# Sixteen of 22 chunks of the last down projection by Strassen's algorithm

## The chip, the core and the metric

The kernel runs as one program on one core of a Trainium2 chip. The core has a matrix engine (PE in the profile; its weight loads are listed apart as PEld), a vector engine (DVE), an activation engine (ACT), a general-purpose engine (POOL), and DMA queues, all of which are issued here from the sync engine's queue (SPq). The engines run beside each other and wait for one another through semaphores. Each takes its instructions in the order in which they were laid out when the program was built. The metric is the time of one execution on the device in microseconds (us); less is better.

## The reference

Two layers of a decoder trunk on 512 tokens of 1024 features. What matters here is the end of the second layer and the norm behind it, all in float32:

```
        h = rms_norm(x, norm2_g[layer]) * (1 + scale2) + shift2
        u = causal_depthwise_conv(h @ w_up[layer], conv_w[layer], conv_b[layer])
        u_gate, u_val = jnp.split(u, 2, axis=-1)
        x = x + gate2 * ((jax.nn.silu(u_gate) * u_val) @ w_down[layer])
    return rms_norm(x, final_g)
```

The activations silu(u_gate) * u_val are 512 tokens by 2816 features; w_down is 2816 by 1024.

## The kernel before

**Precision.** [...] A product of two operands is then three matmuls (high by high, low by high, high by low). `split` makes the parts of a tile of weights: ACT copies it into the high tile `wh` (L566), DVE subtracts into the low tile `wl` (L567). `hilo` does the same for activations (L703 on ACT, L705 or L707 on DVE). There are three buffers for raw weights (`st`) and two each for `wh` and `wl`.

**The feed-forward stage.** `ffn` runs over 22 chunks of 128 features (`NF`). For each it makes two up projections of 24 matmuls (L650 to L652), the three-tap convolution (L1366 to L1368, ACT then DVE), the gate (L1371 to L1373), and with `hilo` the two tiles `act` (high and low, 128 features by 512 tokens). Beside it run the sums of the gate modulation, whose weights are loaded from `w_mod` into tiles `wr`, and `by_tokens`, which loads the residual stream into tiles `x`, transposes it on PE (L535) and writes it back by tokens.

**The last stage.** `last_residual` computes the down projection with tokens on the partitions. A half is 512 of the 1024 output columns; each half is a call of `proj_steps`: for each pair of chunks one tile of weights of 256 rows by 512 columns (512 KB) is loaded and split, and each of four blocks of 128 tokens takes three matmuls per chunk into its own PSUM bank. That is 22 x 4 x 3 = 264 matmuls of 512 columns a half, all at L607 and, for the last eight chunks of the second half, at L581 to L583, where the weights stay in tiles `wr` and the blocks are finished one after the other. `ev` then evacuates a block: DVE multiplies by the gate row (L1330) and adds to the residual (L1331), ACT squares and sums (L1332), DVE multiplies by the norm's gain (L1334 in the first half, L1339 in the second); in the second half follow the small steps of the norm (L1336, L1337 on DVE, L1338 on POOL), the scaling (L1340 on ACT, L1341 on DVE) and two DMAs of the output (L1343).

**Order.** The build lays out each engine's instructions itself, from the program's order and its own estimate of when each can start; the few places that are fixed by hand (`in_order`) are not in the last stage. An engine that stands at a wait holds everything behind it.

Of the kernel before, what the change touches and what calls it, by code (L numbers as in the profile page):

```python
# [23 lines left out]
DFF = 2816  # L24
NF = DFF // P
NU = 2 * NF
NCMP = 31
NEG = -1e30
EPS = 1e-6
# [4 lines left out]
EARLY = (0, NF, 1, NF + 1)  # L34
# [61 lines left out]
def together(*gens):  # L96

    gens = list(gens)
    while gens:
        for g in list(gens):  # L100
            if next(g, gens) is gens:
                gens.remove(g)


class Trunk:
# [5 lines left out]
                   s16=4, hid=1, hidT=1, w2=1, vc=1, den=8, nm=8),  # L111
        "ME": dict(yy=20, m=16),
        "FF": dict(act=44, x=9, wr=16),
        "ST": dict(macc=8, ms=20, ws=16),
    }
    ALL = (mybir.EngineType.PE, mybir.EngineType.DVE, mybir.EngineType.Activation)
# [1193 lines left out]
                M[1].append(lo)  # L1310
        return M

    def last_residual(self, src, Hs, row, rtag):
# [5 lines left out]
        rows, ss = {}, self.t("x", [P, NB, 3])  # L1319
        for half in range(2):  # L1320

            def ev(b, p):
                if not rows:
                    rows["gate"] = self.row_bc(row, "x")
                    rows["gain"] = self.row_bc(io["final_g"], "x")
                x = self.x[b, half]
                s = ss[:, b]
                for i, c in enumerate((slice(0, 256), slice(256, 512)) if half else (slice(0, 512),)):
                    t = self.t("tmp", [P, 512])
                    nc.vector.tensor_tensor(t[:, c], p[:, c], rows["gate"][half][:, c], op=ALU.mult)  # L1330
                    nc.vector.tensor_add(x[:, c], x[:, c], t[:, c])  # L1331
                    nc.scalar.activation(t[:, c], x[:, c], AF.Square, scale=D ** -0.5, accum_out=s[:, half + i:half + i + 1])  # L1332
                if half == 0:
                    nc.vector.tensor_tensor(x, x, rows["gain"][0], op=ALU.mult)  # L1334
                    return
                nc.vector.tensor_tensor(s[:, 0:1], s[:, 0:1], s[:, 1:2], op=ALU.add)  # L1336
                nc.vector.tensor_scalar(s[:, 0:1], s[:, 0:1], s[:, 2:3], EPS, op0=ALU.add, op1=ALU.add)  # L1337
                nc.gpsimd.tensor_tensor(s[:, 0:1], s[:, 0:1], self.nhalf, op=ALU.pow)  # L1338
                nc.vector.tensor_tensor(x, x, rows["gain"][1], op=ALU.mult)  # L1339
                nc.scalar.activation(self.x[b, 0], self.x[b, 0], AF.Copy, scale=s[:, 0:1])  # L1340
                nc.vector.tensor_scalar(x, x, s[:, 0:1], None, op0=ALU.mult)  # L1341
                for e in range(2):
                    nc.sync.dma_start(io["out"][0, b * P:(b + 1) * P, e * 512:e * 512 + 512], self.x[b, e])  # L1343

            yield from self.proj_steps(src, [(half * 512, half * 512 + 512)], Hs, ev, tags=("mm", "at")[half],
                                       resident=8 * half, rtag=rtag, order=((0,), (1,), (2,), (3,)))
# [5 lines left out]
    def ffn(self, l, H, act, early):  # L1352
        nc, io = self.nc, self.io
        W = io["w_up"][l]
        for j in range(NF):
            u2 = self.t("wr", [P, 2, S])
            for e, col in enumerate((j, NF + j)):
                p = early.get(col)
                if p is None:
                    p = self.pt("mm")  # L1360
                    with self.in_order(self.ALL) if j == 2 else nullcontext():
                        w = self.w_tok(W, 0, KD, [(col * P, col * P + P)], P)
                    for k in range(KD):
                        self.mm3f(p, w[0][:, k], w[1][:, k], H[0][k], H[1][k], k == 0, k == KD - 1)
# [12 lines left out]
            act[1].append(lo)  # L1377
            yield

    def run(self):  # L1380
        nc, io = self.nc, self.io
        self.setup()
        AB = self.new_AB()
        for l in range(DEPTH):
            with self.scope("Y"):
                if l == 0:

                    with self.scope("ST"):
# [95 lines left out]
            with self.scope("FF"):  # L1484
                act = ([], [])
                gate2, row = self.new_gate(), self.gate_row() if l + 1 == DEPTH else None
# [5 lines left out]
                mods, ffn = chain(*mods), self.ffn(l, H, act, dict(zip(EARLY, early)))  # L1492
                for j, _ in enumerate(ffn):
                    for _ in range(2 if j in (4, 8, 12, 16, 20) else 1):
                        next(mods, None)
                    next(back, None)
                if l + 1 < DEPTH:
                    pc = []
                    gate1, ABn = self.new_gate(), self.new_AB()
                    mods = chain(self.mod_gate(l + 1, 0, gate1, None, 1024, ("wr", "wr")), self.mod_affine(l + 1, 1, ABn, 0, 1024, ("wr", "wr")))  # L1500
                    H = self.add_norm(io["w_down"][l], act, gate2, AB, "x", 1, 2, lambda H: self.cmp_proj(l + 1, H, ("wr", "wr"), pc), mods)
                    together(mods)
                else:
                    together(self.last_residual(io["w_down"][l], act, row, "wr"))


@with_exitstack
# [27 lines left out]
```

## Time and profile before

| | |
|---|---|
| time, median of 3 runs | 1721.5 us (1721.31 to 1725.55) |
| the profiled execution's own time | 1719.86 us |
| its span, first to last instruction | 1717.8 us |
| PE busy in the span | 1673.8 us (97%) |
| DVE busy | 1195.0 us (70%) |
| ACT busy | 837.3 us (49%) |
| last stage, first matmul to the end of the last | 1590.3 to 1710.1 us |
| from there to the end of the span | 7.6 us |

A matmul is shown busy for longer than the time until the next one starts, since they overlap; what a matmul costs in a dense stretch is the distance between starts. The same holds for DVE and ACT to a lesser degree, so their instructions are counted here by that distance too. [...]

### The profile page before, as it was taken

What the parts mean: (1) busy time and instruction counts of PE and PEld (TensorE: products, weight loads), DVE (VectorE), ACT (ScalarE), POOL (GpSimd) and SP (SyncE); (2) the same over time, 40 slices, a digit from 0 to 9 for tenths busy, and PEclk for the clock granted to TensorE, in tenths of its full rate; (3) what the DMA queues carried; (4) which work ended last, traced back from release to release, by engine and by line L of the source; (5) the groups of instructions that cost most, each with busy time, mean ns of one, the idle gap of its engine ahead of it and who ended that gap; (6) DMA issues with size and microseconds to landing.
All of it is one profiled execution on the core that took longest, in us unless ns stands there. A gap on an engine that the chain in (4) does not pass through costs nothing.

```text
span 1717.8 us, 23192 instructions
## 1 busy us (share of the span) xinstructions
PE 1673.8 (97%) x8469; PEld 1417.4 (83%) x8469; DVE 1195.0 (70%) x2278; ACT 837.3 (49%) x1638; POOL 58.1 (3%) x112
## 2 busy tenths in 40 slices
PE   6999999999999999999999999999999999999998
PEld 4799977878788888887789998778788988888886
DVE  6777768877858888776566646688876686666343
ACT  5455446777434444442334546467754444444222
POOL 3300001000000000000000000100000000000000
PEclk9999999999999999999999999999999999999999
DMA  9547432111544454467534241221146353433322
GB/s 303 172 142 235 136 111 59 49 44 56 172 153 160 159 159 151 156 199 245 186 89 121 81 121 60 53 65 41 43 140 191 127 175 108 144 95 108 134 95 85
DMA packets 274352, 220.09 MB, mean 128 GB/s; under 512 B 25481, under 2 KB 236081, under 8 KB 273983
## 3 DMA queue, kind: packets, MB, share of 16 engines
q1 hardware_dynamic: 273663, 217.57, 40.9%
q8 instruction: 66, 1.08, 0.2%
q10 hardware_dynamic: 576, 1.05, 0.2%
q14 instruction: 47, 0.39, 0.1%
HBM read 205.87 MB, written 12.71 MB: 127 GB/s over the span
## 4 chain that ended last, share of the span: by engine, by line
PE 86%; DVE 5%; DMA 3%; ACT 3%; issue 1%; SPq 0%; POOL 0%; POOLq 0%; DVEq 0%; ACTq 0%
PE pmm L607 20%; PE pmm L650 15%; PE pmm L651 15%; PE pmm L652 15%; PE pat L607 2%; PE pat L1191 2%; DMA wr<-in_w_mod_dram 2%; PE pat L1208 2%; PE pat L652 1%; PE pat L650 1%; PE pat L651 1%; ACT p L699 1%; PE pat L821 1%; DVE wl L567 1%; PE pat L581 1%
## 5 line engine op out<-in xcount | busy, mean ns | idle before, releaser
L567 DVE TENSOR_TENSOR wl<-st,wh 128x1024 fp32r<-128x1024 f32 (+3 forms) x269 | 284.2, 1058 | 194.0 <-ACT wh L566 110.1
L566 ACT ACTIVATE wh<-st 128x1024 fp32r<-128x1024 f32 (+3 forms) x269 | 249.0, 927 | 328.5 <-PE pmm L651 161.1
L650 PE MATMUL pmm<-h,wh 128*128 128x512 f32 x896 | 354.8, 396 | 0.1
L652 PE MATMUL pmm<-h,wl 128*128 128x512 f32 x896 | 350.4, 391 | 1.0 <-DVE wl L567 1.0
L651 PE MATMUL pmm<-h,wh 128*128 128x512 f32 x896 | 349.8, 390 | 0.0
L607 PE MATMUL pmm<-wh,h 128*128 128x512 f32 (+1 forms) x832 | 215.6, 396 | 3.5 <-DVE a L1008 2.1
L652 PEld LDWEIGHTS pmm<-h,wl 128*128 128x128 f32 x896 | 168.2, 188 | 37.9 <-DVE wl L567 2.5
L650 PEld LDWEIGHTS pmm<-h,wh 128*128 128x128 f32 x896 | 168.4, 188 | 32.9 <-ACT wh L566 0.8
L651 PEld LDWEIGHTS pmm<-h,wh 128*128 128x128 f32 x896 | 168.5, 188 | 32.2
L607 PEld LDWEIGHTS pmm<-wh,h 128*128 128x128 f32 x832 | 170.5, 246 | 17.2 <-DVE a L1008 3.8
L607 PE MATMUL pmm<-wl,h 128*128 128x512 f32 (+1 forms) x416 | 104.9, 385 | 0.0
L607 PEld LDWEIGHTS pmm<-wl,h 128*128 128x128 f32 x416 | 85.8, 245 | 5.9
L703 ACT ACTIVATE act<-wr 128x512 fp32r<-128x512 f32 x44 | 27.8, 632 | 110.7 <-DVE wr L1373 110.6
L699 ACT ACTIVATE p<-p,nm 128x128 f32<-128x128 f32 (+3 forms) x128 | 70.8, 554 | 21.1 <-DVE nm L697 20.3
L244 DVE SCALAR_TENSOR_TENSOR wr<-wr,silc,wr 128x1024 f32<-128x1024 f32 x49 | 62.7, 1280 | 13.8 <-DMA wr<-in_w_mod_dram 13.5
L697 DVE CUSTOM_DVE_ANT_0 p<-pat,cst 128x128 f32<-128x128 f32 (+2 forms) x192 | 61.3, 371 | 14.2 <-PE pat L583 8.1
L1366 ACT ACTIVATE wr<-pmm,cols 128x512 f32<-128x512 f32 x88 | 66.7, 763 | 6.9 <-PE pmm L652 5.7
L650 PE MATMUL pmm<-act,wh 128*128 128x512 f32 (+1 forms) x186 | 69.3, 373 | 0.6 <-DVE x L465 0.6
L652 PE MATMUL pmm<-act,wl 128*128 128x512 f32 (+1 forms) x186 | 69.2, 372 | 0.2 <-DVE wl L567 0.2
L651 PE MATMUL pmm<-act,wh 128*128 128x512 f32 (+1 forms) x186 | 69.0, 371 | 0.0
L1367 DVE SCALAR_TENSOR_TENSOR wr<-pmm,cols,wr 128x511 f32<-128x511 f32 x88 | 65.2, 744 | 3.9 <-ACT wr L1366 3.6
L1371 ACT ACTIVATE tmp<-wr 128x512 f32<-128x512 f32 x44 | 27.8, 633 | 81.3 <-DVE wr L1368 65.6
(379 smaller groups left out, 3133.8 us busy)
## 6 DMA issues: line engine op xcount, KB each, us to landing
st<-in_w_up_dram SPq DMA_DIRECT2D x80, 512.0 KB, 3.8
st<-in_w_in_dram SPq DMA_DIRECT2D x124, 256.0 KB, 2.9
wr<-in_w_mod_dram SPq DMA_DIRECT2D x56, 512.0 KB, 5.1
st<-in_w_down_dram SPq DMA_DIRECT2D x38, 512.0 KB, 4.7
st<-in_w_in_dram SPq DMA_DIRECT2D x26, 512.0 KB, 3.4
mss<-in_w_mod_dram SPq DMA_DIRECT2D x48, 256.0 KB, 2.9
ms<-in_w_mod_dram SPq DMA_DIRECT2D x16, 512.0 KB, 6.5
st<-in_w_out_dram SPq DMA_DIRECT2D x16, 512.0 KB, 3.3
```

Source lines behind the costliest of these rows:

```text
L244: nc.vector.scalar_tensor_tensor(acc, w[:, k - k0], self.sc[:, k:k + 1], acc, op0=ALU.mult, op1=ALU.add)
L566: self.nc.scalar.activation(hi, st, AF.Copy)
L567: self.nc.vector.tensor_sub(lo, st, hi.bitcast(F32))
L607: self.nc.tensor.matmul(ps[b][:, :N], H[x][k0 + e][:, s], w[y][:, e, :], start=k0 + e + i == 0, stop=k0 + e + i == nk + 1)
L650: nc.tensor.matmul(out, wh, hh, start=first, stop=False)
L651: nc.tensor.matmul(out, wh, hl, start=False, stop=False)
L652: nc.tensor.matmul(out, wl, hh, start=False, stop=last)
L697: nc.vector.tensor_tensor_reduce(out=pout, in0=ps, in1=mask, scale=-0.125, scalar=3e38, op0=ALU.add, op1=ALU.min, accum_out=negm)
L699: nc.scalar.activation(pout, pout, AF.Exp, bias=negm, scale=-1.0, accum_out=den)
L1191: nc.tensor.transpose(p[:, h * P:(h + 1) * P], src(h), self.ident)
L1366: nc.scalar.activation(u, p, AF.Identity, scale=self.cwc(l, 2, col), bias=self.cbc(l, col))
L1367: nc.vector.scalar_tensor_tensor(u[:, 1:], p[:, :S - 1], self.cwc(l, 1, col), u[:, 1:], op0=ALU.mult, op1=ALU.add)
```

## The change

Of the 22 chunks, the first 16 (`KH` = 8 twice) now go through Strassen's algorithm in Winograd's form. The activations of these chunks are cut into four quarters: by halves of the 16 chunks and by halves of the 512 tokens. The weights are cut likewise: by halves of the chunks and of the output columns. Seven products of sums of quarters, instead of eight products of quarters, give the result. A product is 8 chunks x 2 blocks x 3 = 48 matmuls of 512 columns. The six chunks that are left (`remainder`) are computed as before, 72 matmuls a half of the columns, into the same or into separate PSUM banks.

The parts that it consists of:

- In the feed-forward stage the first 16 chunks are stored unsplit in tiles `ra`, and their `hilo` is dropped. `quarter_sums`, run beside it, makes sums of quarters on DVE, splits the first product's operand (tiles `ah`), and loads four pairs of weight tiles to make their difference `t3` (the order listings call these tiles `t`). The factor one half of the gate moves into the gate row.
- In the last stage a weight tile serves 12 matmuls in a product, not 24, and 24 still in the remainders. Operands of the six other products are split there by `hilo`, two groups of four chunks each, into four buffers `ah`. Products t1, t2 and -t4 need a DVE addition or subtraction for every weight tile, t1 two loads for each.
- The results of products are copied or added on ACT and DVE (`m1`, `m7`, `u3`) and evacuated by `residual`, which is `ev` for one block. The sequence of PE is: products 11, t3, 21, the first remainder, products t2, t1, -t4, the second remainder, product 22.

The core of the diff:

```diff
+    def quarter_sums(self, W):
...
+        for j in range(NF):
+            if j % 3 == 1 and len(self.t3) < KH // 2:
+                s = len(self.t3)
+                t = self.w_quarter(W, 1, 1, s, "t3")
+                nc.vector.tensor_sub(t, t, self.w_quarter(W, 0, 1, s, "wr"))
+                self.t3.append(t)
+            for g, end in enumerate(range(3, KH, 4)):
+                a, z = self.ra[0][g], self.ra[1][g]
+                if j == end:
+                    self.a11.append(self.split_group(a[:, :, h0]))
+                if j == KH + end:
+                    s1 = self.t("sa", [P, 4, S // 2])
+                    nc.vector.tensor_add(s1, a[:, :, h1], z[:, :, h1])
+                    nc.vector.tensor_sub(a[:, :, h1], a[:, :, h0], a[:, :, h1])
+                    nc.vector.tensor_sub(a[:, :, h0], s1, a[:, :, h0])
...
+        def weights(name, s):
+            if name in ("11", "21", "22"):
+                return self.w_quarter(W, int(name[0]) - 1, int(name[1]) - 1, s, "st")
+            if name == "t1":
+                w = self.w_quarter(W, 0, 1, s, "st")
+                nc.vector.tensor_sub(w, w, self.w_quarter(W, 0, 0, s, "wr"))
+                return w
+            if name == "t2":
+                nc.vector.tensor_add(t3[s], t3[s], self.w_quarter(W, 0, 0, s, "st"))
+            if name == "-t4":
+                nc.vector.tensor_sub(t3[s], self.w_quarter(W, 1, 0, s, "st"), t3[s])
+            return t3[s]
+        def mms(ps, blocks, a, w, n, first, last=False):
+            for i, (x, y) in enumerate(((0, 0), (1, 0), (0, 1))):
+                for k in range(n):
+                    for b in blocks:
+                        nc.tensor.matmul(ps[b], a[x](k, b), w[y][:, k], ...)
+        def product(ps, A, name, first):
+            A = list(A)
+            for s in range(KH // 2):
+                a = operand(A, s)
+                w = self.split(weights(name, s), [P, 2, S])
+                mms(ps, range(2), a, w, 2, first and s == 0, s == KH // 2 - 1)
...
+        product(p1, A12, "21", False)
+        pr = pair("at")
+        remainder(p1 + pr, 0, (False, True))
+        for b in range(2):
+            t = self.t("tmp", [P, S])
+            nc.vector.tensor_tensor(t, pr[b], gate[0], op=ALU.mult)
+            nc.vector.tensor_add(self.x[2 + b, 0], self.x[2 + b, 0], t)
+        for b in range(2):
+            residual(b, 0, p1[b], 0)
+        product(p7, quarter(0, h0), "t2", False)
...
+        product(p5, self.s1, "t1", True)
...
+        product(p7, A22, "-t4", False)
+        for b in range(2):
+            nc.vector.tensor_add(m1[b], p7[b], m1[b])
+            residual(2 + b, 0, m1[b], 0)
+        pr = pair("at")
+        remainder(p5 + pr, 1, (False, True))
+        for b in range(2):
+            nc.vector.tensor_add(u3[b], pr[b], u3[b])
+            residual(2 + b, 1, u3[b], 1)
+            t = self.t("tmp", [P, S])
+            nc.vector.tensor_tensor(t, m7[b], gate[1], op=ALU.mult)
+            nc.vector.tensor_add(self.x[b, 1], self.x[b, 1], t)
+        ws, ops, A12 = [], [], list(A12)
+        for s in range(KH // 2):
+            ops.append(operand(A12, s))
+            ws.append(self.split(weights("22", s), [P, 2, S], ("wr", "wr") if s else ("wh", "wl")))
+            if s < 1:
+                mms(p5, range(2), ops[s], ws[s], 2, False)
+        for b in range(2):
+            for s in range(1, KH // 2):
+                mms(p5, (b,), ops[s], ws[s], 2, False, s == KH // 2 - 1)
+            residual(b, 1, p5[b], 1)
...
-            nc.vector.tensor_tensor(uv, uv, t, op=ALU.mult)
-            hi, lo = self.t("act", [P, S], F32R), self.t("act", [P, S], F32R)
-            self.hilo(uv, hi, lo, 0.5)
-            act[0].append(hi)
-            act[1].append(lo)
+            if raw and j < 2 * KH:
+                nc.vector.tensor_tensor(raw(j), uv, t, op=ALU.mult)
+            else:
+                nc.vector.tensor_tensor(uv, uv, t, op=ALU.mult)
+                hi, lo = self.t("act", [P, S], F32R), self.t("act", [P, S], F32R)
+                self.hilo(uv, hi, lo, 1.0 if raw else 0.5)
```

Where instructions now stand. On DVE, before the change, at the end of the first half: the evacuation of the first half's blocks (`pmm` to `tmp`, then `h`) with a weight split (`wl`) among it.

```order
L1334 TENSOR_TENSOR h_15004<-h_15004,x_15355 128x512
L1331 TENSOR_TENSOR h_15008<-h_15008,tmp_15369 128x512
L1330 TENSOR_TENSOR tmp_15374<-pmm_15020,x_15351 128x512
L567 TENSOR_TENSOR wl_15416<-st_15413,wh_15415 128x1024
L1334 TENSOR_TENSOR h_15008<-h_15008,x_15355 128x512
```

On DVE, after the change, at the end of the first remainder: `pat` and `pmm` are the four finished banks; `wl_15374` is the low part of product t2's second weight tile, and the row ahead of the eight evacuation rows makes a weight tile of product t1.

```order
L1379 TENSOR_TENSOR st_15489<-st_15489,wr_15491 128x1024
L1453 TENSOR_TENSOR tmp_15331<-pat_15239,x_14993 128x512
L1453 TENSOR_TENSOR tmp_15334<-pat_15240,x_14993 128x512
L1454 TENSOR_TENSOR h_14984<-h_14984,tmp_15331 128x512
L1454 TENSOR_TENSOR h_14988<-h_14988,tmp_15334 128x512
L1427 TENSOR_TENSOR tmp_15337<-pmm_15003,x_14993 128x512
L1427 TENSOR_TENSOR tmp_15342<-pmm_15004,x_14993 128x512
L1428 TENSOR_TENSOR h_14976<-h_14976,tmp_15337 128x512
L1428 TENSOR_TENSOR h_14980<-h_14980,tmp_15342 128x512
L569 TENSOR_TENSOR wl_15374<-t_2933_13621,wh_15373 128x1024
```

All eight evacuation rows of the first remainder stand ahead of the second weight's low part.

On ACT, before the change, in the last stage there are only weight copies in a row (`wh`), one for each 24 matmuls:

```order
L566 ACTIVATE wh_15263<-st_15261 128x1024
L566 ACTIVATE wh_15293<-st_15291 128x1024
L566 ACTIVATE wh_15323<-st_15321 128x1024
L566 ACTIVATE wh_15385<-st_15383 128x1024
L566 ACTIVATE wh_15415<-st_15413 128x1024
```

On ACT, after the change, in product -t4: `wh_15542`, `15561`, `15584`, `15603` are its four weight tiles, `ah_15577` the high part of its second operand group, `ah_15763` that of the first operand group of product 22, the last one.

```order
L568 ACTIVATE wh_15542<-t_2889_13357 128x1024
L705 ACTIVATE ah_15577<-ra_13300 128x1024
L568 ACTIVATE wh_15561<-t_2933_13621 128x1024
L705 ACTIVATE ah_15763<-ra_13299 128x1024
L568 ACTIVATE wh_15584<-t_2983_13900 128x1024
L568 ACTIVATE wh_15603<-t_3019_14136 128x1024
```

The operand of product 22, which takes an `ah` buffer that product -t4 still reads, stands ahead of -t4's third weight tile.

## Rows read from the trace of the kernel before

**Rows 1.** The page, busy time, share of the span and instructions of each engine

```profile
PE 1673.8 (97%) x8469; PEld 1417.4 (83%) x8469; DVE 1195.0 (70%) x2278; ACT 837.3 (49%) x1638; POOL 58.1 (3%) x112
```

**Rows 2.** Stretches: busy us and counts by engine, granted clock, DMA share, GB/s

```profile
1375.00:1590.30 215.30, 215.30 (x964) 177.58 (x963) 152.03 (x186) 96.82 (x129) 0.00 (x0) 1.00 0.41 126
1590.30:1650.20 59.90, 59.90 (x266) 49.41 (x265) 17.54 (x18) 13.79 (x14) 0.00 (x0) 1.00 0.34 122
1650.20:1710.20 60.00, 59.90 (x265) 49.26 (x263) 26.73 (x46) 17.12 (x32) 2.72 (x3) 1.00 0.24 83
```

**Rows 3.** Chain that ended last, in order of time: start us, us, what

```profile
1590.30 59.96 PE pmm L607 x264
1650.26 38.08 PE pat L607 x168
```

**Rows 4.** Waits, 1560 to the end: waiter <- releaser: us in total, times, longest

```profile
ACT wh L566 <- PE pmm L607: 42.7, 10, 4.4
DVE wl L567 <- PE pmm L607: 37.6, 9, 4.2
```

**Rows 5.** DVE's timeline in the last stage: start us, us, line, operation

```profile
1648.94 1.29 DVE L1330 TENSOR_TENSOR tmp<-pmm,x 128x512 f32<-128x512 f32 x2 [2.80 <-PE pmm L607]
1650.14 1.29 DVE L1331 TENSOR_TENSOR h<-h,tmp 128x512 f32<-128x512 f32 x2
1651.35 0.69 DVE L1330 TENSOR_TENSOR tmp<-pmm,x 128x512 f32<-128x512 f32 x1
...
1656.89 1.22 DVE L567 TENSOR_TENSOR wl<-st,wh 128x1024 fp32r<-128x1024 f32 x1
1658.03 0.68 DVE L1334 TENSOR_TENSOR h<-h,x 128x512 f32<-128x512 f32 x1
```

**Rows 6.** ACT's timeline in the last stage

```profile
1670.24 1.06 ACT L566 ACTIVATE wh<-st 128x1024 fp32r<-128x1024 f32 x1 [4.33 <-PE pat L607]
```

**Rows 7.** DVE's timeline from the last matmul to the end

```profile
1710.14 0.76 DVE L1330 TENSOR_TENSOR tmp<-pat,x 128x256 f32<-128x256 f32 x2 [1.59 <-PE pat L583]
1710.81 0.75 DVE L1331 TENSOR_TENSOR h<-h,tmp 128x256 f32<-128x256 f32 x2
1711.86 0.16 DVE L1336 TENSOR_TENSOR x<-x 128x1 f32<-128x1 f32 x1 [0.30 <-ACT tmp L1332]
...
1713.51 0.49 DVE L1341 TENSOR_SCALAR h<-h,x 128x512 f32<-128x512 f32 x1 [0.44 <-POOL x L1338]
```

**Rows 8.** DMA issues of the last stage: count, KB each, median us to landing

```profile
st<-in_w_down_dram SPq DMA_DIRECT2D x18, 512.0 KB, 3.5
```

**Rows 9.** Groups by line and form in the feed-forward stage: busy us, mean ns | idle

```profile
L567 DVE TENSOR_TENSOR wl<-st,wh 128x1024 fp32r<-128x1024 f32 x39 | 47.8, 1225 | 35.7 <-ACT wh L566 35.7
L707 DVE SCALAR_TENSOR_TENSOR act<-wr,act 128x512 fp32r<-128x512 f32 x20 | 13.8, 691 | 12.6 <-ACT act L703 12.6
L703 ACT ACTIVATE act<-wr 128x512 fp32r<-128x512 f32 x20 | 12.6, 632 | 50.3 <-DVE wr L1373 50.3
```

**Rows 10.** All of PE's waits from 1350 to 1717 us

```profile
PE pat L535 <- DMA x<-xd: 1.2, 2, 0.7
```

**Rows 11.** PE's timeline in the first 60 us, matmuls behind a wait

```profile
30.67 6.44 PE L607 MATMUL pmm<-ws,h 128*128 128x512 f32 x20 [1.91 <-ACT h L703]
42.97 5.78 PE L607 MATMUL pmm<-ws,h 128*128 128x512 f32 x24 [2.80 <-ACT h L703]
```

**Rows 12.** Stretches in the first 60 us, same columns as rows 2

```profile
10.00:20.00 10.00, 9.41 (x67) 8.32 (x68) 8.47 (x22) 4.81 (x13) 2.09 (x4) 1.00 1.12 349
30.00:35.00 5.00, 4.33 (x12) 3.42 (x13) 5.00 (x10) 5.00 (x17) 4.61 (x7) 0.66 0.79 223
45.00:50.00 5.00, 5.00 (x24) 4.13 (x23) 4.86 (x10) 4.36 (x13) 3.48 (x6) 1.00 0.75 274
50.00:55.00 5.00, 2.40 (x16) 2.08 (x14) 3.99 (x15) 4.41 (x11) 2.00 (x4) 0.98 0.61 164
```

More of the change, by code (lines that the diff above doesn't have):

```diff
@@ L1318, in last_residual @@
                 self.load_x(b, half)
[L1319 to L1346, printed above, removed]
@@ new lines, in last_residual @@
+        ss = self.t("x", [P, NB, 3])
+        gate, gain = self.row_bc(row, "x"), self.row_bc(io["final_g"], "x")
+        for g in gate:
+            nc.vector.tensor_scalar(g, g, 0.5, None, op0=ALU.mult)
+        h0, h1 = slice(0, S // 2), slice(S // 2, S)
+        quarter = lambda kh, c: [x[:, :, c] for x in self.ra[kh]]
+        t3 = self.t3
+        def weights(name, s):
[4 more added lines that the diff above has]
+                nc.vector.tensor_sub(w, w, self.w_quarter(W, 0, 0, s, "wr"))
+                return w
+            if name == "t2":
[3 more added lines that the diff above has]
+            return t3[s]
@@ new lines, in mms, with operand @@
+        def mms(ps, blocks, a, w, n, first, last=False):
+            for i, (x, y) in enumerate(((0, 0), (1, 0), (0, 1))):
+                for k in range(n):
+                    for b in blocks:
+                        nc.tensor.matmul(ps[b], a[x](k, b), w[y][:, k], start=first and k + i == 0, stop=last and k + i == n + 1, skip_group_check=True)
+        def operand(A, s):
+            g, o = s // 2, s % 2 * 2
+            if s % 2 == 0:
+                A[g] = A[g] if isinstance(A[g], tuple) else self.split_group(A[g])
+            return [lambda k, b, x=x: x[:, o + k, b * P:(b + 1) * P] for x in A[g]]
@@ new lines, in product, with remainder @@
+        def product(ps, A, name, first):
[4 more added lines that the diff above has]
+                mms(ps, range(2), a, w, 2, first and s == 0, s == KH // 2 - 1)
+        def remainder(ps, nh, first):
+            n = NF - 2 * KH
+            for k in range(0, n, 2):
+                st = self.t("st", [P, 2, S])
+                r = (2 * KH + k) * P
+                nc.sync.dma_start(st, W[r:r + 2 * P, nh * S:nh * S + S].rearrange("(k p) c -> p k c", p=P))
+                a = [lambda e, b, x=x: x[k + e][:, b * P:(b + 1) * P] for x in rest]
+                w = self.split(st, [P, 2, S])
+                for blocks, new in zip((range(2), range(2, NB)), first):
+                    mms(ps, blocks, a, w, 2, new and k == 0, k == n - 2)
@@ new lines, in last_residual, with residual @@
+        pair = lambda tag: [self.pt(tag) for _ in range(2)]
+        copy = lambda ps: [self.copied(p) for p in ps]
+        def residual(b, half, p, last):
+            x, s = self.x[b, half], ss[:, b]
+            for i, c in enumerate((slice(0, 256), slice(256, 512)) if last else (slice(0, 512),)):
+                t = self.t("tmp", [P, 512])
+                nc.vector.tensor_tensor(t[:, c], p[:, c], gate[half][:, c], op=ALU.mult)
+                nc.vector.tensor_add(x[:, c], x[:, c], t[:, c])
+                nc.scalar.activation(t[:, c], x[:, c], AF.Square, scale=D ** -0.5, accum_out=s[:, last + i:last + i + 1])
+            if not last:
+                nc.vector.tensor_tensor(x, x, gain[half], op=ALU.mult)
+                return
+            nc.vector.tensor_tensor(s[:, 0:1], s[:, 0:1], s[:, 1:2], op=ALU.add)
+            nc.vector.tensor_scalar(s[:, 0:1], s[:, 0:1], s[:, 2:3], EPS, op0=ALU.add, op1=ALU.add)
+            nc.gpsimd.tensor_tensor(s[:, 0:1], s[:, 0:1], self.nhalf, op=ALU.pow)
+            nc.vector.tensor_tensor(x, x, gain[half], op=ALU.mult)
+            nc.scalar.activation(self.x[b, 1 - half], self.x[b, 1 - half], AF.Copy, scale=s[:, 0:1])
+            nc.vector.tensor_scalar(x, x, s[:, 0:1], None, op0=ALU.mult)
+            for e in range(2):
+                nc.sync.dma_start(io["out"][0, b * P:(b + 1) * P, e * 512:e * 512 + 512], self.x[b, e])
@@ new lines, in last_residual @@
+        A12, A22 = quarter(1, h0), quarter(1, h1)
+        p1, p7 = pair("mm"), pair("mm")
+        product(p1, self.a11, "11", True)
+        m1 = copy(p1)
+        product(p7, quarter(0, h1), "t3", True)
+        m7 = copy(p7)
+        product(p1, A12, "21", False)
[5 more added lines that the diff above has]
+            nc.vector.tensor_add(self.x[2 + b, 0], self.x[2 + b, 0], t)
@@ new lines, in last_residual @@
+        for b in range(2):
+            residual(b, 0, p1[b], 0)
+        product(p7, quarter(0, h0), "t2", False)
+        u3 = [self.t("h", [P, S]) for _ in range(2)]
+        for b in range(2):
+            nc.vector.tensor_add(u3[b], p7[b], m1[b])
+            nc.vector.tensor_sub(m7[b], u3[b], m7[b])
+        p5 = pair("at")
+        product(p5, self.s1, "t1", True)
+        for x, y in zip(A12, quarter(0, h0)):
+            nc.vector.tensor_sub(x, x, y)
+        for b in range(2):
+            nc.vector.tensor_add(u3[b], p5[b], u3[b])
@@ L1491, in run @@
                 back = self.by_tokens("x") if l + 1 == DEPTH else iter(())
-                mods, ffn = chain(*mods), self.ffn(l, H, act, dict(zip(EARLY, early)))
+                mods, ffn = chain(*mods), self.ffn(l, H, act, dict(zip(EARLY, early)), raw)
                 for j, _ in enumerate(ffn):
@@ L1496, in run @@
                     next(back, None)
+                    next(sums, None)
                 if l + 1 < DEPTH:
@@ L1503, in run @@
                 else:
-                    together(self.last_residual(io["w_down"][l], act, row, "wr"))
+                    self.last_residual(io["w_down"][l], act, row)
 @with_exitstack
```

34 lines of the change are left out of this document (31 added, 3 removed).

## Prediction

> **What bounds the kernel now.** The page comes first: PE is busy for 97% of the span [rows 1], which says little by itself, because matmuls overlap in this listing. So the last stage is read next, by itself. In its two halves PE is busy throughout and DVE for 29% and 45% [rows 2]. The chain that ended last shows what a matmul costs there: 264 of them take 59.96 us, one piece with no gap, so 0.227 us each [rows 3]; the second half begins at 1650.26 and its first evacuation behind the last matmul at 1710.14 [rows 3, 7], the same 0.227. The waits agree: ACT and DVE wait for PE, 4.4 and 4.2 us at a time, to give back the buffers `wh` and `wl` [rows 4]; PE itself waited from 1350 us on only twice, 1.2 us together, at the start of the feed-forward stage [rows 10]. So the last stage is 528 matmuls long, then 7.6 us of norm and output. What the reader is to see: each matmul taken away is worth 0.227 us as long as ACT and DVE keep ahead, and they now have much room. The question is how much of that room the change uses up.
>
> [...]
>
> **What is removed.** The matmuls of 16 chunks go from 8 to 7 products of 48: 384 to 336. With the 144 of the remainders the stage has 480 in place of 528. 48 x 0.227 = 10.9 us less, if PE never waits. The columns of a matmul and the forms of its operands are as before, so the 0.227 should hold.
>
> **What is added on DVE and ACT in the last stage.** Durations are taken as distances between starts in a dense row: on DVE 1.14 us for 1024 columns (1656.89 to 1658.03), 0.60 for 512 (1648.94 to 1650.14 for two; also from PSUM) [rows 5], 0.335 for 256 (1710.14 to 1710.81 for two) [rows 7]; on ACT 1.06 us for 1024 [rows 6]. DVE's instructions of 1024 columns are then: 34 weight splits (before 22), 12 sums of weight tiles (t1, t2, -t4), 12 operand splits, 2 sums of operands: 60 x 1.14 = 68 us. Evacuation and sums of results are 34 of 512 and 16 of 256 columns, 20 + 5 us, and some 3 us of small steps. Together 96 us beside 109 us of PE. On average it fits. It doesn't fit everywhere: a weight tile now lasts PE 12 matmuls, 2.72 us, and in products t2, t1 and -t4 it costs DVE a sum, a split and half an operand split, 1.14 + 1.14 + 0.57 = 2.85 us. Three products in a row are slightly DVE-bound, and evacuation comes on top.
>
> So PE's waits are worked out at the three places that the order shows.
>
> (a) Behind the first remainder all eight evacuation rows stand ahead of the low part of t2's second weight. They can start when the last matmul has ended, one distance of 0.23 behind its start: 0.23 + 8 x 0.60 + 1.23 until that low part is written = 6.3 us. PE comes to it 21 starts later, 12 matmuls of the first weight and 8 of the second between: 4.8 us. PE waits **1.5 us**.
>
> (b) From there to the last low part of -t4 the DVE order holds 20 instructions of 1024 and 8 of 512 columns: 22.8 + 4.8 = 27.6 us. PE has 120 matmuls in that time, 27.2 us. Two of these rows wait for the end of product t2, some 0.5 us. Between 0.4 (everything hidden but the excess) and 1.9 us (each further dependency in series, too); end to end along the three orders I get **1.2**.
>
> (c) In -t4 ACT's copy `ah_15763` stands ahead of the third weight's `wh_15584`, and it takes the buffer of the second operand's low part, which PE reads for the last time in the eighth of the second weight's 12 matmuls. From that start: 0.23 + 1.06 + 1.06 = 2.4 us on ACT, against 5 starts, 1.1 us, on PE. PE waits **1.2 us**, whatever DVE does.
>
> Together 3.9 us. Low end 1.9, if (b) and (c) overlap. High end 9: the sums wait for loads as well, and a load takes 3.5 us from issue to landing [rows 8] with three buffers `st`. From t2 to -t4 there are 16 loads, 8.4 MB, in about 33 us, 255 GB/s; the old stage moved 122 and 83 [rows 2]. At the start of the kernel 349 GB/s is held for 10 us, later 223 to 274 in slices [rows 12]. I take no cost, nearest to the 349, since that is the row in which loads of this size stand in a queue; at 274 I get 1 us more and at 223 about 5.
>
> **The tail.** Behind the second remainder's last matmul DVE has, ahead of the last product's first block: 2 + 4 + 2 of 512 columns, 8 of 256, two scalings of 0.4 and four small steps, 4.8 + 2.7 + 0.8 + 0.4 = 8.7 us. That block is finished after 12 + 18 matmuls, 6.8 us; DVE comes 1.9 us late. The second block is finished 18 matmuls, 4.1 us, later, and the first one's chain takes DVE 2.6 us plus its waits for ACT and POOL (3.9 us in all in [rows 7]): 0.4 to 1.7 us late. I add **1.1 us** to the 7.6 (0 to 2; the four output blocks leave closer together, too).
>
> **The feed-forward stage.** DVE loses 16 low parts of 0.69 and ACT 16 high parts of 0.63 [rows 9]; DVE gains 12 instructions of 1.22 (four t3, six sums, two splits), ACT two: 11.0 out, 14.7 in, on 152 busy of 215 us [rows 2]. The cover is DVE's 63 idle us and PE's distance from them: PE didn't wait there after the first loads [rows 10]. 4.2 MB more are loaded over the 215 us, 126 to 146 GB/s. The weak place is the start, where PE already waits 1.2 us for `x` [rows 10] and SP gets the loads of t3 among those of the modulation. I take **0.4 us**, between -0.5 (the wait for x falls, as the loads are laid out anew) and 2 (it doubles, and a split waits behind a t3 that isn't there yet).
>
> **The sum.** -10.9 + 3.9 + 1.1 + 0.4 = -5.5 us. The span goes from 1717.8 to 1712.3, the profiled execution's own 1719.86 to 1714.4; the median of the runs is 1.6 us above that execution, so the forecast is 1721.5 - 5.5 = **1716.0 us**. By the ends of the terms: -10.9 + 1.9 + 0 - 0.5 = -9.5 and -10.9 + 9 + 2 + 2 = +2; both at once are unlikely.
>
> **The rivals.**
>
> 1. *ACT and DVE stay hidden.* If PE runs through t2 to -t4 without a wait, only tail and start count: -10.9 + 1.5 = -9.4, **1712**. For it: 96 us of DVE work beside 109. Against it: (a) and (c) are in the order itself. 0.10.
>
> 2. *PE's clock falls behind the new waits.* [...] Against it: 24 matmuls behind a wait of 2.80 us took 5.78, 0.24 each, at a clock of 1.00 [rows 11, 12]. Here PE is dense on both sides. 0.14. [...]
>
> 3. *Slower: the loads bind.* 8.4 MB from t2 to -t4 at 164 GB/s, the slice from 50 to 55 us [rows 12], take 51 us, 18 more than PE's 33; the three loads ahead in `st` and those of t1 into `wr` save some 5. 1716.0 + 13 = **1729**. It decides below about 200 GB/s. For it: one queue carries all. Against it: 349 in [rows 12]. 0.06.
>
> 4. [...] 0.03. That the change doesn't remove the matmuls is no rival: the built program has 48 fewer.
>
> **How the numbers follow.** The forecast has 0.67, with an uncertainty of about 1.5 us from (b), the tail and the loads. A measurement of this kernel tells a change from none at about 0.3%, 5.2 us, that is below 1716.3 or above 1726.7. The forecast lies just beyond the first bound: 0.40 of its 0.67 faster, 0.27 the same. Rival 1 is faster (0.10), rival 2 the same (0.14), rivals 3 and 4 slower (0.09). Faster 0.50, same 0.41, slower 0.09. The range leaves out rivals 3 and 4 and the outer tails of 1 and 2: 1712 to 1720.5.
>
> **What would show it.** In the profile after: the stage from the first matmul of product 11 to the last is near 113 us and not 109; PE's waits there are of ACT `wh` and DVE `wl`, three or four of 0.4 to 1.5 us, the first 5 us behind the first remainder, for DVE. DVE is busy without a gap from the end of the first remainder to the second. The granted clock stays at 1.00. The end comes 8.7 us after the last matmul. I would be wrong if PE waited for a DMA in the stage (rival 3), if a stretch of it had a clock below 0.9 (rival 2), if PE waited for `wl` in the feed-forward stage, or if a DVE sum in quarter views or in place took longer than the 1.14 us that a split takes.

## The result and the profile after

The changed kernel takes 1731.66 us (median of 6 runs, 1727.87 to 1733.96), the kernel before 1722.15 beside it: 1.0052 times as long, 95% interval 1.0038 to 1.0067. It is about 9 us **slower**, where 5.5 us less were forecast, and lies outside the range of 1712 to 1720.5. The profiled execution took 1727.87 us, its span is 1726.1.

The page's first part and the list of all of PE's waits from 1360 to 1720 us of the kernel after (waiter <- releaser: us in total, times, longest), to be held against [rows 1, 10]:

```profile
PE 1668.9 (97%) x8421; PEld 1411.1 (82%) x8421; DVE 1252.7 (73%) x2332; ACT 857.1 (50%) x1652; POOL 58.7 (3%) x112
...
PE pmm L654 <- DVE wl L569: 4.0, 1, 4.0
PE pmm L1391 <- DVE wl L569: 2.8, 2, 2.1
PE pmm L1391 <- ACT wh L568: 1.4, 2, 1.2
PE pat L537 <- DMA x<-xd: 1.0, 2, 0.6
```

The 48 matmuls are gone (8469 to 8421). L1391 is the last stage: its waits come to 4.2 us, where 3.9 were forecast. The first of the rows of waits is new and was not forecast at all: one wait of 4.0 us at L654, in the feed-forward stage, for the low part of a weight.

PE's starts divide the end of the kernel into three parts. The mark ahead of them is the four one-column matmuls `pat<-idn,dq` of the norm before the feed-forward stage, which both kernels have. PE's timeline of before, then of after, at the mark:

```profile
1346.25 0.50 PE L401 MATMUL pat<-idn,dq 128*128 128x1 f32 x4
```

```profile
1349.84 0.50 PE L403 MATMUL pat<-idn,dq 128*128 128x1 f32 x4
```

| us | before | after | difference | forecast |
|---|---|---|---|---|
| from the mark to the last stage's first matmul | 243.9 | 249.4 | +5.5 | +0.4 |
| last stage, first to last matmul's start | 119.6 | 115.8 | -3.8 | -7.0 |
| last matmul's start to the end of the span | 8.1 | 11.1 | +3.0 | +1.1 |
| start to the mark, nothing changed there | 1346.2 | 1349.8 | +3.6 | 0 |

The last line is no effect of the change: in ten profiles of eight kernels with the same code up to there, the mark stood between 1346.25 and 1353.60 us, and the unaltered kernel before, profiled a second time, had it at 1349.71 (the run before_again, below). So all that follows is counted from the mark.

**The wait in the feed-forward stage.** DVE's timeline of the kernel after (start us, us, line, operation, idle before and what ended it), and PE's around the wait:

```profile
1454.46 0.75 DVE L1517 SCALAR_TENSOR_TENSOR wr<-pmm,cols,wr 128x510 f32<-128x510 f32 x1
1464.94 0.43 DVE L1368 TENSOR_SCALAR x<-x 128x512 f32<-128x512 f32 x1 [9.73 <-DMA x<-gd]
1465.29 0.68 DVE L1523 TENSOR_TENSOR ra<-wr,tmp 128x512 f32<-128x512 f32 x1
1465.89 0.42 DVE L1368 TENSOR_SCALAR x<-x 128x512 f32<-128x512 f32 x1
1466.22 1.22 DVE L569 TENSOR_TENSOR wl<-st,wh 128x1024 fp32r<-128x1024 f32 x1
```

```profile
1463.06 0.39 PE L653 MATMUL pmm<-h,wh 128*128 128x512 f32 x1
1467.49 0.80 PE L654 MATMUL pmm<-h,wl 128*128 128x512 f32 x1 [4.04 <-DVE wl L569]
1468.09 0.63 PE L652 MATMUL pmm<-h,wh 128*128 128x512 f32 x1
1468.52 0.63 PE L653 MATMUL pmm<-h,wh 128*128 128x512 f32 x1
```

L1368 is the new instruction that multiplies the gate row by 0.5, in two halves. In the code it stands at the head of `last_residual`; in DVE's order it stands in the middle of the feed-forward stage. It waits 9.73 us for the gate row, and DVE takes nothing past it: the product of the chunk and the low part `wl`, for which PE then waits 4.04 us, stand behind. The matmuls behind the wait start 0.43 us apart and not 0.227; the stretch from 1467.4 to 1471 us (busy us and counts by engine, granted clock of PE as a share of full speed, DMA share, GB/s) has a clock of 0.54:

```profile
1467.40:1471.00 3.60, 3.50 (x9) 2.80 (x10) 2.56 (x5) 2.03 (x3) 0.00 (x0) 0.54 0.78 256
```

That is 1.6 us lost in eight starts (3.42 us from 1467.49, and not 1.81), on top of the wait.

SP's order of the same kernel shows how long the row is under way: from the write of the gate's column to memory to the read that spreads it over the partitions.

```profile
1449.88 0.36 SPq L367 DMA_DIRECT2D gd<-gcol  x1
1459.51 0.81 SPq L374 DMA_DIRECT2D x<-gd  x2
```

In after_again, the same kernel once more (below), the chain of work that ended last runs through both (start us, us, what):

```profile
1447.53 9.19 DMA gd<-gcol
1456.74 5.36 DMA x<-gd
```

The kernel before has these two transfers at the same place, 10.3 us apart. There nothing reads the row until the last stage. SP's order of before:

```profile
1446.62 0.36 SPq L365 DMA_DIRECT2D gd<-gcol  x1
1456.96 0.81 SPq L372 DMA_DIRECT2D x<-gd  x2
```

### The profile page after: what moved, and what is told of

Same layout as the page of the kernel before. It is cut to its first block, busy times and chain, and to the rows that moved or that the text cites. A ratio compares the mean times of both kernels' runs of the same rounds, so it can differ in the third digit from the quotient of the medians.

```text
span 1726.1 us, 23204 instructions
## 1 busy us (share of the span) xinstructions
PE 1668.9 (97%) x8421; PEld 1411.1 (82%) x8421; DVE 1252.7 (73%) x2332; ACT 857.1 (50%) x1652; POOL 58.7 (3%) x112
## 3 DMA queue, kind: packets, MB, share of 16 engines
q10 hardware_dynamic: 576, 1.05, 0.2%
## 4 chain that ended last, share of the span: by engine, by line
PE 72%; DVE 6%; DMA 4%; ACT 3%; issue 1%; POOL 0%; SPq 0%; POOLq 0%; DVEq 0%; ACTq 0%
PE pmm L652 15%; PE pmm L654 15%; PE pmm L653 15%; PE pmm L609 9%; PE pmm L1391 3%; PE pat L1193 2%; PE pat L1210 2%; PE pat L654 1%; PE pat L652 1%; PE pat L653 1%; DVE wl L569 1%; DMA mss<-in_w_mod_dram 1%; DMA wr<-in_w_mod_dram 1%; DMA st<-in_w_down_dram 1%; ACT p L701 1%
## 5 line engine op out<-in xcount | busy, mean ns | idle before, releaser
L654 PE MATMUL pmm<-h,wl 128*128 128x512 f32 x896 | 351.4, 392 | 4.0 <-DVE wl L569 4.0
L654 PEld LDWEIGHTS pmm<-h,wl 128*128 128x128 f32 x896 | 168.6, 188 | 41.3 <-DVE wl L569 5.9
L246 DVE SCALAR_TENSOR_TENSOR wr<-wr,silc,wr 128x1024 f32<-128x1024 f32 x49 | 62.8, 1281 | 14.7 <-DMA wr<-in_w_mod_dram 14.4
L699 DVE CUSTOM_DVE_ANT_0 p<-pat,cst 128x128 f32<-128x128 f32 (+2 forms) x192 | 61.4, 371 | 14.1 <-PE pat L585 8.1
L654 PE MATMUL pmm<-act,wl 128*128 128x512 f32 (+1 forms) x186 | 69.6, 374 | 0.3 <-DVE wl L569 0.3
L1517 DVE SCALAR_TENSOR_TENSOR wr<-pmm,cols,wr 128x510 f32<-128x510 f32 x88 | 65.5, 748 | 2.5
```

What stands on the lines that cost most here:

```text
L246: nc.vector.scalar_tensor_tensor(acc, w[:, k - k0], self.sc[:, k:k + 1], acc, op0=ALU.mult, op1=ALU.add)
L654: nc.tensor.matmul(out, wl, hh, start=False, stop=last)
L699: nc.vector.tensor_tensor_reduce(out=pout, in0=ps, in1=mask, scale=-0.125, scalar=3e38, op0=ALU.add, op1=ALU.min, accum_out=negm)
```

## The experiments

Kernels of one group ran on one chip beside the kernel before, which had 1722.83 us there in the first four (29 runs) and 1722.42 in the second four (20 runs).

**gate_small.** The factor goes onto the gate's column of 128x8, before it is written to memory:

```diff
         if row is not None:
+            nc.vector.tensor_scalar(gc, gc, 0.5, None, op0=ALU.mult)
             nc.sync.dma_start(row.rearrange("(k p) -> p k", p=P), gc)
...
-        for g in gate:
-
-            nc.vector.tensor_scalar(g, g, 0.5, None, op0=ALU.mult)
```

> The changed kernel, with the factor 0.5 put on the gate's 128x8 column before it is written to memory, so that no instruction of VectorE in the feed-forward stage reads the gate row. Theory A (the two scalings of the gate row stood at the head of VectorE's queue and waited 9.7 us for the row's transfer, which cost TensorE a wait of 4.0 us and 1.6 to 1.8 us at a lower clock behind it): 5.8 us less than the changed kernel, about 1726 us; no TensorE wait above 0.5 us between 1380 and 1590 us. Rival B (the extra loads and sums of the feed-forward stage cost it, the wait falls on another instruction): no more than 1 us less, about 1731.

Measured: 1725.32 us (12 runs), ratio 1.0013, interval 1.0004 to 1.0022. The kernel after has 1.0052; by the medians, 6.3 us less. The kernel is still 2.5 us above the one before. From the mark to the last stage 244.2 us pass, as in before. All of PE's waits from 1360 to 1720 us:

```profile
PE pmm L1389 <- DVE wl L570: 3.6, 2, 2.9
PE pat L538 <- DMA x<-xd: 1.4, 2, 1.1
PE pmm L1389 <- ACT wh L569: 1.4, 2, 1.2
```

None is left in the feed-forward stage but that for `x`, which [rows 10] has too. The other instructions of the change there (four t3, six sums, two splits, 4.2 MB) cost nothing that shows. Theory A holds, B falls.

**before_gate_early.** The scaling, with the requests of both rows moved ahead of it in the code, in the kernel before (here by 1.0):

```diff
+        rows = {"gate": self.row_bc(row, "x"), "gain": self.row_bc(io["final_g"], "x")}
+        for g in rows["gate"]:
+            nc.vector.tensor_scalar(g, g, 1.0, None, op0=ALU.mult)
...
-                if not rows:
-                    rows["gate"] = self.row_bc(row, "x")
-                    rows["gain"] = self.row_bc(io["final_g"], "x")
```

> The kernel before, with only this taken over from the change: gate row and gain row are requested at the head of the last stage's code and the gate row's two halves are multiplied by a number on VectorE there (here by 1.0). Theory A: the scalings land in the middle of the feed-forward stage and wait for the transfer there too, about 5.8 us more than the kernel before, 1728 us. Rival B: within 1 us of the kernel before, 1722.

Measured: 1729.86 us (6 runs), ratio 1.0047 (1.0033 to 1.0061), 7.0 us more than before. DVE's timeline, ACT's, PE's first matmul behind, and the stretch from 1466 to 1480 us:

```profile
1469.05 0.43 DVE L1322 TENSOR_SCALAR x<-x 128x512 f32<-128x512 f32 x1 [9.63 <-DMA x<-gd]
```

```profile
1470.11 0.63 ACT L703 ACTIVATE act<-wr 128x512 fp32r<-128x512 f32 x1 [12.24 <-DVE wr L1373]
```

```profile
1471.74 0.80 PE L650 MATMUL pmm<-h,wh 128*128 128x512 f32 x1 [4.54 <-ACT wh L566]
```

```profile
1466.00:1480.00 14.00, 9.42 (x28) 6.75 (x27) 8.71 (x12) 4.98 (x7) 0.00 (x0) 0.76 0.68 195
```

The wait passes through two engines here: ACT waits for the product that stands behind the scaling on DVE (L1373), and PE waits for the weight copy that stands behind that on ACT. The requests themselves stay in SP's order where the kernel before has them, 10.1 us behind the write, and gate_small has them early in the code at no cost; so it is the two instructions of 0.43 us that make the kernel 7 us slower. In the profile the part from the mark to the last stage is 252.1 us, 8.2 more than before: 4.5 of wait and 3.4 in 14 matmuls at a lower clock behind it (0.76 on the mean of the stretch). One part alone gives about what undoing it gives back, and theory A is shown from both sides.

**evac_spread.** As gate_small, and the evacuation of the first remainder is written between the weight tiles of t2:

```diff
...
-        product(p7, quarter(0, h0), "t2", False)
+        evacuate = [lambda b=b: add_pr(b) for b in range(2)] + [lambda b=b: residual(b, 0, p1[b], 0) for b in range(2)]
+        product(p7, quarter(0, h0), "t2", False, [lambda: None] + evacuate[:3])
+        evacuate[3]()
```

> As gate_small, and the eight evacuations behind the first remainder are written one by one behind the weight tiles of product t2 in place of all ahead of the second one. Theory A for the last stage (TensorE's wait of about 2 us behind the first remainder and the lower clock behind it cost 2 to 4 us): 2 to 4 us less than gate_small, about 1723, and the granted clock from 1650 to 1660 us above 0.95. Rival C (VectorE is short of time over t2, t1 and -t4 as a whole, 27.6 us beside 27.2; what is moved comes back as waits later): within 1 us of gate_small, and the waits stand in product -t4.

Measured: 1721.74 us (11 runs), ratio 0.9990 (0.9981 to 1.0000), 3.6 us less than gate_small. The stretch from 1650 to 1660 us, of gate_small, then of evac_spread:

```profile
1650.00:1660.00 10.00, 8.67 (x31) 7.00 (x32) 7.68 (x9) 5.12 (x9) 0.00 (x0) 0.83 0.04 7
```

```profile
1650.00:1660.00 10.00, 8.49 (x35) 6.08 (x34) 10.00 (x14) 6.07 (x9) 0.00 (x0) 1.00 0.16 54
```

Both theories have a part in it. The lower clock is gone, as A says. The waits are not: what PE loses over the stage against 0.227 us for each matmul falls only from 7.8 to 6.4 us in the two profiles, since in place of the wait of 2.9 us and three shorter ones there are seven of 0.2 to 1.2 us between 1654 and 1676 us. What is moved comes back as waits later, as C says, though not where C said: the four new waits stand in t1, and the two in -t4 are those of gate_small. DVE is busy for all 10.00 us of the stretch from 1650 us. These two profiles differ by 0.7 us in stage and tail together, as C has it, the medians by 3.6, as A has it; single executions of the kernels with the long wait differ by as much (below). How much of the 3.6 the stage gives is therefore not shown.

**sums_early.** As evac_spread, and the sums for t2 and t1 are made during the first remainder:

```diff
+        def early_sums():
+            for s in range(KH // 2):
+                u = self.w_quarter(W, 0, 0, s, "st")
+                nc.vector.tensor_add(t3[s], t3[s], u)
+                w = self.w_quarter(W, 0, 1, s, "wr")
+                nc.vector.tensor_sub(w, w, u)
+                t1.append(w)
+                yield
...
             for k in range(0, n, 2):
+                if k:
+                    next(ahead, None)
+                    next(ahead, None)
```

> As evac_spread, and the eight sums of weight tiles for t2 and t1 are made during the first remainder, where VectorE has only one split for each 24 matmuls. Theory A: the waits of the last stage but one of about 1.3 us in -t4 go, with the clock steady at 1.00 there; last stage about 110 us to its last matmul, total about 1717 to 1719, below the kernel before. Rival C': the stage stays above 114 us, since loads or clock and not VectorE's queue set it; total 1723 or more. Rival D (fewer matmuls are not worth 0.227 us each): not below the kernel before.

Measured: 1719.59 us (12 runs), ratio 0.9983 (0.9973 to 0.9994). From the first to the last matmul of the stage 111.8 us, of which 3.05 lost. PE's two waits there:

```profile
1635.88 2.11 PE L1385 MATMUL pmm<-wh,act 128*128 128x512 f32 x8 [1.31 <-ACT wh L569]
...
1670.04 2.12 PE L1385 MATMUL pmm<-wh,ah 128*128 128x512 f32 x8 [1.19 <-ACT wh L569]
```

The waits for `wl` in t2 to -t4 are gone, as A says; the wait of 1.2 us for ACT in -t4, which A wanted gone too, stays, and the one at 1635.88 us, in the first remainder, is new. The stage is 1.8 us longer than A's 110. It is below 114 us and the kernel below the one before, so C' and D fall: 479 distances of 0.227 make 108.7 us, and the 3.05 above that are lost at these two waits alone; everywhere else the starts are 0.227 us apart. The worth of a matmul stood the test.

**after_again, before_again.** Both kernels unaltered.

> The changed kernel once more, unaltered. In the first pair of profiles the part that both kernels have in common (to 1347 us) took 3.6 us longer in the changed one, and the medians lie 9.5 us apart where the stages account for some 5. Theory A (that part varies from one execution to the next, whatever the kernel): the part ends anywhere from 1347 to 1355 us in the new profile; median 1727 to 1732; the feed-forward wait of 4 us and the wait of 2 to 3 us behind the first remainder are there again. Rival E (the changed program is slower there each time): the part ends at 1350.5 us or later again, and the median is 1731 or more.

> The kernel before once more, unaltered, as a measure of what two measurements of one kernel differ by. Theory A: 1721 to 1725 us, ratio 1.000 within 0.001, and the part up to the feed-forward stage ends within a range of some us, not at 1347.3 us again. Rival E: it ends within 1 us of 1347.3.

Measured: after_again 1730.19 us (5 runs), ratio 1.0052 (1.0038 to 1.0066); before_again 1721.73 us (11 runs), ratio 1.0000 (0.9992 to 1.0009). The mark stands at 1346.96 us in after_again, and at 1349.71 in before_again: the other way round than in the first pair. The common part varies whatever the kernel (A). The feed-forward wait is there again (3.5 us, 249.5 us from mark to stage). The wait behind the first remainder is 3.7 us this time in place of 2.1.

**act_ordered, blocks_reversed.** As sums_early, and ACT's copy of the last product's operand is held behind the weights of -t4; then, in the second of them, the second remainder also takes blocks 2 and 3 first:

```diff
-        product(p7, A22, "-t4", False)
+        with self.in_order((mybir.EngineType.Activation,)):
+            product(p7, A22, "-t4", False)
...
+        with self.in_order((mybir.EngineType.Activation,)):
+            A12[0] = self.split_group(A12[0])
...
-                for blocks, new in zip((range(2), range(2, NB)), first):
+                for blocks, new in list(zip((range(2), range(2, NB)), first))[::1 - 2 * nh]:
```

> As sums_early, and ScalarE's copy of the last product's first operand is kept behind the weight copies of product -t4. Theory A: TensorE's wait of 1.3 us for a weight copy in -t4 falls to about 0.8 or less, so 0.5 to 1.3 us less than sums_early, 1718.5; TensorE's starts behind the other wait stay 0.227 us apart. Rival F (the wait is of the operand's own copy, which only comes later): the same wait stands elsewhere, time as sums_early, 1719.6.

> As act_ordered, and in the second remainder the matmuls of blocks 2 and 3 come ahead of those of blocks 0 and 1, so that VectorE can begin their evacuation 12 matmuls, 2.7 us, earlier. Theory A (the tail of 11 us in place of 8 is VectorE's queue: the evacuation of blocks 2 and 3 keeps the last product's first block waiting): from the last matmul's start to the end 9 to 10 us in place of 11.7, so 1.5 to 2.5 us less than act_ordered, about 1716.5. Rival G (the tail is the chain ACT, POOL and DVE within each block): within 0.5 us of act_ordered.

Measured: act_ordered 1718.79 us (9 runs), ratio 0.9977 (0.9967 to 0.9986). The wait in -t4 went from 1.2 to 0.8 us; the 0.8 us between the medians of sums_early and act_ordered are within their spread, so the sign rests on the trace alone. Theory A holds for this wait. blocks_reversed 1717.61 us (6 runs), ratio 0.9971 (0.9959 to 0.9982), 4.8 us below the kernel before and 12.6 below after_again on the same chip. Its tail is 8.1 us, as in before, where act_ordered has 11.6: theory A of the tail holds, which had 9 to 10, and G falls by the trace. The medians lie only 1.2 us apart, less than A's 1.5 to 2.5. The edit does more than bring the blocks forward: DVE begins their evacuation 2.3 us ahead of the end of the remainder and not 1.6 us behind it, since the last low part of product 22 (`wr`), which waits for a load (see the tail, below), now stands behind it. A new wait for that low part takes 0.9 us back; PE's timeline of blocks_reversed:

```profile
1703.79 4.40 PE L1385 MATMUL pat<-wr,ah 128*128 128x512 f32 x18 [0.86 <-DVE wr L570]
```

## Why the prediction was wrong, step by step

The steps in us against the kernel before, from the two profiles of the changed kernel:

| step | forecast | after | after_again |
|---|---|---|---|
| 48 matmuls fewer | -10.9 | -10.9 | -10.9 |
| (a) behind the first remainder | +1.5 | +4.0 | +6.4 |
| (b) and (c), t2 to -t4 | +2.4 | +2.6 | +2.5 |
| smaller losses of PE in the stage | 0 | +0.5 | +1.1 |
| tail | +1.1 | +3.0 | +4.0 |
| feed-forward stage | +0.4 | +5.5 | +5.6 |
| sum | -5.5 | +4.7 | +8.7 |

**The feed-forward stage failed, by 5.1 us, the largest miss.** By itself it would have brought the sum to about zero (-5.5 + 5.1); that the kernel became slower took (a) and the tail as well. The step counted DVE's instructions (11.0 us out, 14.7 in) and set them against 63 idle us. It left out the two of L1368, the cheapest of the new ones, and asked of none what it waits for and who stands behind. What was missing is a wait, which no sum of durations holds. The trace of before had it to see: the write of the gate's column lands 10.3 us after its issue and the read waits for it. The text named the sign of this error, PE waiting for `wl` there, without its cause; a clock below 0.9 in the last stage, its sign for rival 2, came as well. What the wait cost is shown by gate_small and before_gate_early.

**(a) had the right place and was mis-sized: 1.5 us were forecast, 4.0 and 6.4 lost.** Its working was right, with an end missing on each side. The evacuation takes 6.01 us from its first start to the low part written; 6.03 was forecast. But it was to start 0.23 us behind the last matmul of the remainder. DVE's timelines of after and then of after_again:

```profile
1644.36 1.22 DVE L1379 TENSOR_TENSOR st<-st,wr 128x1024 f32<-128x1024 f32 x1 [1.09 <-DMA st<-in_w_down_dram]
1645.51 1.22 DVE L569 TENSOR_TENSOR wl<-t,wh 128x1024 fp32r<-128x1024 f32 x1
1646.64 2.35 DVE L1379 TENSOR_TENSOR st<-st,wr 128x1024 f32<-128x1024 f32 x2
1648.91 1.28 DVE L1453 TENSOR_TENSOR tmp<-pat,x 128x512 f32<-128x512 f32 x2
...
1653.70 1.22 DVE L569 TENSOR_TENSOR wl<-t,wh 128x1024 fp32r<-128x1024 f32 x1
```

```profile
1641.34 1.23 DVE L1382 TENSOR_TENSOR t<-t,st 128x1024 f32<-128x1024 f32 x1 [1.63 <-DMA st<-in_w_down_dram]
1643.52 1.23 DVE L1379 TENSOR_TENSOR st<-st,wr 128x1024 f32<-128x1024 f32 x1 [0.95 <-DMA st<-in_w_down_dram]
...
1648.35 1.28 DVE L1453 TENSOR_TENSOR tmp<-pat,x 128x512 f32<-128x512 f32 x2
```

Three sums of t1 (L1379) stand ahead of it as well, and they and those of t2 (L1382) wait for loads, up to 1.6 us at a time. The remainder's last matmul starts at 1647.93 us in after and 1645.80 in after_again, so the evacuation begins 0.98 and 2.55 us behind it, 0.75 and 2.3 late; PE's waits of 2.1 and 3.7 us are about the 1.5 us of the forecast and this lateness. This is rival 3, the loads, in small: PE never waits for one in the stage, but they put DVE's queue back, and by different amounts in each execution. They are issued late: of the 14.1 us that SP's queue waits from 1628 to 1650 us in after, 11.8 are for DVE to give back buffers. Two of these loads are in the chain of work that ended last, one ahead of the wait at (a), one ahead of the tail (kernel after):

```profile
1639.43 4.84 DMA st<-in_w_down_dram
1654.98 8.06 PE pmm L1391 x27
...
1699.33 3.66 DMA st<-in_w_down_dram
1709.14 1.48 POOL x L1435
```

That the loads are what differs between the two executions is read from these rows; no run took them alone away.

On the other side stands the clock (rival 2), the stretches behind the wait in after, then in after_again:

```profile
1654.90:1659.40 4.50, 4.42 (x12) 3.58 (x13) 4.50 (x6) 1.56 (x2) 0.00 (x0) 0.62 0.00 0
```

```profile
1654.40:1659.70 5.30, 5.28 (x12) 4.13 (x13) 4.57 (x5) 1.50 (x2) 0.00 (x0) 0.50 0.00 0
```

Twelve matmuls that need 2.72 us took 4.47 and 5.29: 1.75 and 2.6 us lost at a granted clock of 0.62 and 0.50. The rival was right at (a), and in the feed-forward stage; at (c) it was wrong: from 1676 to 1684 us of after, where 0.85 and 1.36 us are lost to waits, the clock is 1.00:

```profile
1676.00:1684.00 8.00, 6.11 (x26) 4.41 (x25) 8.00 (x9) 2.96 (x3) 0.00 (x0) 1.00 0.55 182
```

Its chance of 0.14 rested on PE being dense on both sides, which did not help. No run shows a time to go with that chance; the traces show the 1.75 and 2.6 us behind (a), and a clock of 1.00 at (c). In evac_spread seven short waits stand within 22 us, at a clock of 1.00 as well. The stretch of evac_spread:

```profile
1654.00:1676.00 22.00, 17.81 (x71) 12.79 (x71) 21.81 (x24) 10.85 (x12) 0.00 (x0) 1.00 0.46 156
```

The chances also count 0.03 for rival 4, by which the matmuls taken away give nothing; no run shows a ground for it. In its place sums_early shows starts 0.227 us apart everywhere but at its two waits, and a time of 0.9983 of the kernel before.

**(c) was right, and (b) right in its size only.** At (c) 1.36 us are lost, behind the copy that was named. For (b) 0.35 and 0.85 us are lost, 1.2 as forecast, but not because DVE was short of time: behind (a) PE had lost 2.5 us more than forecast, and DVE stood idle twice from 1659 to 1663 us, for 1.25 and 1.05 us. The 0.35 is a wait for ACT's weight copy in t1. The 0.85 is the first low part of -t4, which stands behind two sums (L1467) that wait for the end of t1. So the agreement in (b) is partly luck; evac_spread, where (a) costs nothing, loses 3.8 us in t1. DVE's and ACT's rows of after for (b) and (c):

```profile
1674.84 1.29 DVE L1467 TENSOR_TENSOR h<-pat,h 128x512 f32<-128x512 f32 x2 [0.19 <-PE pat L1391]
1676.04 2.35 DVE L569 TENSOR_TENSOR wl<-t,wh 128x1024 fp32r<-128x1024 f32 x2
```

```profile
1680.37 1.06 ACT L705 ACTIVATE ah<-ra 128x1024 fp32r<-128x1024 f32 x1 [4.57 <-PE pmm L1391]
```

**The tail was mis-sized.** DVE's part was 8.7 us and took 8.86 (1705.25 to 1714.11). But it was to begin where the second remainder ends, and it began 0.9 us later in after and 1.9 us later in after_again: the low part of product 22's last weight stands ahead of it on DVE, and its high part on ACT had waited for a load. DVE's and ACT's rows of after:

```profile
1704.11 1.23 DVE L569 TENSOR_TENSOR wr<-st,wr 128x1024 fp32r<-128x1024 f32 x1 [2.43 <-ACT wr L568]
```

```profile
1703.02 1.06 ACT L568 ACTIVATE wr<-st 128x1024 fp32r<-128x1024 f32 x1 [2.79 <-DMA st<-in_w_down_dram]
```

So the first block was evacuated 2.9 us late in after, where 1.9 was forecast. Its chain takes 3.5 us, within the bounds. The bounds for the second block's lateness were 0.4 to 1.7 us, and 1.1 lay between them; it came 2.4 us late, 2.2 later than in before, and from its evacuation to the end 8.46 us pass and not 7.64. DVE's timeline of after at the second block:

```profile
1717.62 0.42 DVE L1427 TENSOR_TENSOR tmp<-pat,x 128x256 f32<-128x256 f32 x1
1718.13 0.49 DVE L1438 TENSOR_SCALAR h<-h,x 128x512 f32<-128x512 f32 x1
1718.54 0.42 DVE L1428 TENSOR_TENSOR h<-h,tmp 128x256 f32<-128x256 f32 x1
...
1721.64 0.48 DVE L1438 TENSOR_SCALAR h<-h,x 128x512 f32<-128x512 f32 x1 [0.44 <-POOL x L1435]
```

In [rows 7] the two halves of an evacuation stand next to each other; here the other block's scaling lies between them.

**What stays open.** The ratio of 1.0052 means +9 us (by its interval 6.5 to 11.5), and the sum of after_again, +8.7, meets it; that of after, +4.7, falls short. The profiled executions of the first pair themselves lie 8.0 us apart, of which 3.6 are in the part up to the mark. In both groups the profiled execution was the fastest of the changed kernel's runs (1727.87 and 1729.22 us); whether the others had longer waits at (a) or a later mark isn't shown, since no trace of them is there.

## What to carry to other kernels

Ask of each new instruction, however small, what it waits for and what stands behind it on its engine: two instructions of 0.43 us that had to wait for a transfer cost 7 us, and the same factor applied ahead of the transfer cost nothing that shows. A saving on a busy engine is worth its full price per instruction only if the engine that feeds it is still ahead at its worst place; so spread its evacuations and move its sums to where it is idle, before counting the saving (here +9 us became -4.8, with 6.3 us of it from the gate's factor). A wait of PE in a dense stretch may have slower matmuls behind it and is to be priced with them: behind the waits of 2.1 to 4.5 us in these traces they cost 1.6 to 3.4 us more.

## What the runs showed of the hardware that was not expected

A write of 4 KB from a column of 128x8 to memory, element by element (1056 packets under 512 B from 1447 to 1457 us of before), let the read that depends on it wait 9.6 us in after and 10.3 in before; what part of that the small pieces have is not shown. A load of 512 KB landed 3.5 us after its issue in the last stage of before [rows 8].

Behind waits of PE of 2.1, 3.7 and 4.0 us the granted clock was 0.62, 0.50 and 0.54, with PE dense on both sides; around the last stage's waits of up to 1.31 us it stayed at 1.00. The wait of 2.80 us in [rows 11] had no such effect (a clock of 1.00 from 42.9 to 48.8 us of before), and that of 1.91 had (0.66 from 30 to 35 us [rows 12]), so the length of the wait alone doesn't settle it.
